# Trunk of a hybrid encoder: repeated key columns kept in scratch, load and copy order at the attention's start, norm statistics and input casts moved

## The chip, the cores and the metric

The kernel runs on one core of one Trainium2 chip. The metric is device time in microseconds (us) of one execution; the time before is the median of three runs. All times below are from the profile of one execution, from its trace, or from those runs.

## What is computed

One transformer layer runs on two sequences with shared weights: a prompt of 1024 tokens (s=0) and a sample of 512 tokens (s=1), each with 16 meta tokens ahead of it (n = 1040 and 528). The width is 1024, all in 32-bit floats.

```python
def mixer_sublayer(x, ...):
    n = rms_norm(x, g_mix)
    qa, ka, va, qb, kb, vb = jnp.split(n @ w_in, cuts, axis=-1)
    # group A: 8 query heads on 2 key heads of 64, RMS-normed q and k, axial rotary
    oa = softmax(rope(norm(qa)) @ rope(norm(ka)).T * scale) @ va
    # group B: 4 heads, difference of two softmax maps, linear rotary, v of 128
    p  = softmax(qb @ kb.T * scale)                  # two maps per head
    ob = rms_norm((p[0] - lam * p[1]) @ vb, g_subln) * (1 - lam_init)
    return x + concat(oa, ob) @ w_out
def conv_glu_sublayer(x, ...):
    n = rms_norm(x, g_ffn)
    gate = depthwise_conv3(n @ w_ff_gate) + conv_b
    return x + (gelu(gate) * (n @ w_ff_up)) @ w_ff_down
# a last RMSNorm, and the meta tokens are dropped
```

## The kernel before

Every dense product (`dense`, `mm3` at L132 to L134) is three matmuls of split operands: the rounded high part of the data by the high weights, the low part by the high weights, the high part by the low weights. `split` and `load_weight` (L126, L127) make the parts: a cast on ACT (or POOL, L153) gives `_hi`, a subtraction on DVE or POOL gives `_lo`. Weights stream in as `w_f` tiles of 128x1024 on ACT's DMA queue; all other loads and stores are issued by SP, in order.

The program is a set of Python generators that a scheduling function, `merge`, interleaves by weights: `projection(s)` (norm statistics, q, k and v with rotary, stores to scratch in HBM: `qk`, `ka`, `v`, `vt`), `attention(s)` (group A in blocks of 512 queries, then group B in blocks of about 342 or 306 and 208), `mixer_out(s)` (w_out, residual, sum of squares) and `conv_glu(s)`. The stages are: the sample's projection alone; the sample's attention beside the prompt's projection (`R1`, with a lead of `LEAD1` for the projection); the prompt's attention beside the sample's feed-forward (`f1`, `R2`); the prompt's `mixer_out` beside the rest of `f1` (`R3`); the prompt's `conv_glu` alone. Each engine then works through its own list in order: an instruction that waits holds up all that stands behind it on that engine.

Names and places in this text:

- `load_k` (L378, L394): loads 1040 key columns. A softmax reads `nch` equal chunks of an even width `kw`, 3x348 = 1044 columns for the prompt, so POOL copies the first four columns behind the last (L394). For the sample 2x264 = 528 needs no copy.
- `load_q` (L378), `load_v` (L399, and `v_tail`, L401): q, v and the last rows of v. In group A, POOL copies the first two columns of a head's first q block into `halo` (L512).
- `softmax`: scores `ps_s` (L413, L414 on PE), a scale with a running minimum into `p` (L417, DVE), exp (L420, ACT). In group B ACT scales both maps, with the factor `c` from POOL for the second (L545, then L546), and POOL adds them into `p` (L547). `pt_hi` and `pt_lo` are the transposed p (L434 on PE, L126 and L127), multiplied by v at L444 to L448 and L458.
- In `projection`: `x` loads (L193), `xhi` (L195, ACT), `xlo` (L196, DVE), squares (L199, ACT). The prompt's squares are summed into `acc` by POOL (L204), then L214 (PE) and `rsqrt_newton` (L113 to L119) give `rstd`. POOL multiplies the rotary tables by `rstd` (L347); `head_norm` adds `eps2` (L234, POOL) ahead of a matmul (L238).
- In `mixer_out`: `h<-oT` loads (L629), casts `xhi<-h` (L126; L636 on POOL for the sample), the residual add, a square (L589, ACT) and the running sum `acc` (L590, POOL); at the end the mean by a matmul with `ones_d` (L595, PE).

Of the kernel before, what the change touches and what calls it, by code (L numbers as in the profile page):

```python
# [51 lines left out]
def even_chunks(total, cap):  # L52
    cnt = -(-total // cap)
    w = -(-total // cnt)
    w += w % 2
    out, c = [], 0
    while c < total:
        out.append((c, min(w, total - c)))
        c += w
    return out  # L60

# [68 lines left out]
def mm3(g, ps, whi, wlo, xhi, xlo, start, stop):  # L130
    nc = g.nc
    nc.tensor.matmul(ps, lhsT=whi, rhs=xhi, start=start, stop=False)  # L132
    nc.tensor.matmul(ps, lhsT=whi, rhs=xlo, start=False, stop=False)  # L133
    nc.tensor.matmul(ps, lhsT=wlo, rhs=xhi, start=False, stop=stop)  # L134
# [25 lines left out]
def projection(ctx, g, s, side, tag, tag2):  # L160
# [23 lines left out]
    with tc.tile_pool(name=f"ps{s}", bufs=2, side=side, reuse_waits="tile") as sp:  # L184
        if s == 1:
            ms = [g.psum.tile(P, cw, tag2) for _, cw in chunks]
        else:
            acc = sp.tile([P, n], F32, name="acc", bufs=1)
        for k in range(KT):
            for c0, cw in even_chunks(n, 528):  # L190
                cc = slice(c0, c0 + cw)
                x = g.xin.tile([P, 528], F32, name="x", tag="x")[:, :cw]
                nc.sync.dma_start(out=x, in_=g.xT[s][k * P:(k + 1) * P, cc])  # L193
                gk = g.vec[:, V_GMIX + k:V_GMIX + k + 1]
                nc.scalar.activation(xhi[k][:, cc], x, AF.Copy, scale=gk)  # L195
                nc.vector.scalar_tensor_tensor(out=xlo[k][:, cc], in0=x, scalar=gk,  # L196
                                               in1=xhi[k][:, cc].bitcast(F32), op0=ALU.mult, op1=ALU.subtract)
                sq = acc[:, cc] if k == 0 and s == 0 else x
                nc.scalar.activation(sq, x, AF.Square)  # L199
                if s == 1:  # L200
                    for ps, (c1, w) in zip(ms, chunks):
                        nc.tensor.matmul(ps, lhsT=g.ones_d, rhs=x[:, c1:c1 + w], start=k == 0, stop=k == KT - 1)
                elif k:
                    nc.gpsimd.tensor_tensor(out=acc[:, cc], in0=acc[:, cc], in1=x, op=ALU.add)  # L204
        yield 0
        c0, cw = chunks[0]
        first_ps = g.psum.tile(P, cw, tag)
        dense(g, first_ps, first, xhi, xlo, c0, cw)
        for i, (c0, cw) in enumerate(chunks):
            if s == 1:  # L210
                ps = ms[i]
            else:
                ps = g.psum.tile(P, cw, tag2)
                nc.tensor.matmul(ps, lhsT=g.ones_d, rhs=acc[:, c0:c0 + cw], start=True, stop=True)  # L214
            nc.vector.tensor_scalar(out=eps2[:, c0:c0 + cw], in0=ps, scalar1=EPS, scalar2=2 * EPS,
                                    op0=ALU.add, op1=ALU.mult)
            rsqrt_newton(g, sp, rstd[:, c0:c0 + cw], ps, cw)
        nc.vector.tensor_scalar(out=rstd, in0=rstd, scalar1=-0.5, scalar2=None, op0=ALU.mult)
# [3 lines left out]
    tab = load_tables(0)  # L222
# [19 lines left out]
    def finish(y, hn, dst, twice, c0, cw):  # L242

        if hn is not None:
            nc.vector.tensor_tensor(out=y, in0=y, in1=hn[:, None, :].broadcast_to(list(y.shape)), op=ALU.mult)
        hi = tmp(bp, "hi", y.shape[1], cw, 2, F32R)
        lo = y.bitcast(F32R)
        split(g, hi, lo, y, nc.gpsimd)
        for i, part in enumerate((hi, lo, hi) if twice else (hi, lo)):
            to = dst[i, :, :, c0:c0 + cw]  # L250
            to = to.rearrange("x p n -> p x n") if y.shape[1] == 2 else to.rearrange("x p n -> (x p) n")[:, None]
            nc.sync.dma_start(out=to, in_=part.bitcast(F32))

    def pair(j, w=None):
# [4 lines left out]
        for c0, cw in chunks:  # L259
# [16 lines left out]
            finish(y, hn, g.qk[s][PAIRS.index(j)], QB <= j < KB, c0, cw)  # L276

    def keys_a():
        cos, sin = tab
        gk, ngk = scales[KA]  # L280
        for c0, cw in chunks:
            cc = slice(c0, c0 + cw)
            if c0 == 0:
# [14 lines left out]
            finish(y, head_norm(sq, g.ones_hd, c0, cw, HD), g.ka[s], True, c0, cw)  # L298
            yield 25 * cw

    def values(j):
        w = load_weight(g, g.w_in[j], lo_engine=nc.gpsimd)
        dst, tail = g.v[s][0 if j == VA else 1 + j - VB], g.vt[s][0 if j == VA else 1 + j - VB]
        for c0, cw in chunks:
# [11 lines left out]
            for i0, i1, kw in ((0, nf, P), (nf, nt, cw - nf * P)):  # L316
# [11 lines left out]
                if kw == P:  # L328
                    nc.sync.dma_start(out=dst[:, t0 + i0:t0 + i1, :], in_=v.bitcast(F32)[:, i0:i1, :])
# [27 lines left out]
def attention(ctx, g, s, side):  # L357
# [3 lines left out]

    nch = -(-n // 512)
    kw = -(-n // nch)
    kw += kw % 2
# [25 lines left out]
    def load_k(j, m, first=0):  # L390
        k = kp.tile([P, ne], F32R, name="k", tag="k")
        stacked(k[:, :n], j, m, first, 0, n)
        if ne > n:
            nc.gpsimd.tensor_copy(k[:, n:], k[:, :ne - n])  # L394
        return k

    def load_v(i, w, c0):
        v = vp.tile([P, nf, 2 * P], F32R, name="v", tag="v")[:, :, :w]
        nc.sync.dma_start(out=v.bitcast(F32), in_=g.v[s][i][:, :, c0:c0 + w])  # L399
# [181 lines left out]
def add_square(g, tp, acc, h, j, c0, cw, eng, bufs=2):  # L581
# [5 lines left out]
    else:  # L587
        sq = tp.tile([P, cw], F32, name="sq", tag="sq", bufs=bufs)
        nc.scalar.activation(sq, hs, AF.Square)  # L589
        eng.tensor_tensor(out=acc, in0=acc, in1=sq, op=ALU.add)  # L590


def mean_rsqrt(g, tp, out, acc, cw, tag="mm"):
    ps = g.psum.tile(P, cw, tag)
    g.nc.tensor.matmul(ps, lhsT=g.ones_d, rhs=acc, start=True, stop=True)  # L595
# [3 lines left out]
def mixer_out(g, s, st, side, whole, tag):  # L599
# [6 lines left out]
    with ExitStack() as es:  # L606
        mp = pool(es, g, f"fm{s}", 3, side)
        waiting = []

        def finish():  # L610
            while waiting:
                c0, cw, acc = waiting.pop(0)
                mean_rsqrt(g, mp, rstd[:, c0:c0 + cw], acc, cw, tag)

        for group in ([chunks] if whole else [[c] for c in chunks]):
            if whole:
                (xhi, xlo), base = [[x[:, k] for k in range(KT)] for x in st.x], 0
            else:
                xhi = [mp.tile([P, cm], F32R, name="xhi", tag=f"xhi{k}", bufs=2) for k in range(KT)]
                xlo = [mp.tile([P, cm], F32R, name="xlo", tag=f"xlo{k}", bufs=2) for k in range(KT)]  # L620
# [19 lines left out]
            for j in range(KT):  # L640
                w = load_weight(g, g.w_out[j])
                for c0, cw in group:
# [9 lines left out]
                    add_square(g, mp, acc[:, c0 - base:c0 - base + cw], h, j, c0, cw, nc.gpsimd, 1)  # L652
# [127 lines left out]
def merge(a, wa, b, wb, lead=0, tail=False):  # L780
# [4 lines left out]
    while True:  # L785
        i = 0 if b is None or done[0] / wa <= done[1] / wb else 1
        try:
            w = next((a, b)[i])
# [23 lines left out]
LEAD1, LATE = 2 * 24 * 384, 22  # L812
# [3 lines left out]
def trunk_kernel(ctx, tc, g):  # L816
# [5 lines left out]
    for s, N in enumerate(SEQS):  # L822
        n = N + NMETA
        g.qk.append([dram.tile([3, 2, P, n], F32, name=f"qk{s}_{i}") for i in range(len(PAIRS))])
        g.ka.append(dram.tile([3, 2, HD, n], F32, name=f"ka{s}"))
        g.v.append([dram.tile([P, n // P, 2 * P], F32, name=f"v{s}_{i}") for i in range(5)])
# [70 lines left out]
    with ExitStack() as es:  # L897
        g.xin = pool(es, g, "xin", 7, "right")
# [4 lines left out]
    with es0:  # L903
        with ExitStack() as es1:
            merge(attention(es1, g, 1, "right"), R1[0], p0, R1[1], LEAD1)
# [4 lines left out]
    with ExitStack() as es1:  # L910
# [6 lines left out]
        with ExitStack() as es0:  # L917
# [3 lines left out]
            merge(a0, R2[0], f1, R2[1], tail=True)  # L921
        g.psum.relay(s=6)
        st0 = state(ctx, 0, "left", False)
        merge(mixer_out(g, 0, st0, "left", False, "s"), R3[0], f1, R3[1])
# [5 lines left out]
    drain(conv_glu(ctx, g, 0, st0, "right", 2))  # L930
# [64 lines left out]
```

## Time and profile before

| what | value |
|---|---|
| median of 3 runs | 2268.64 us (2266.8 to 2272.45) |
| profiled execution | 2269.33 us, its span in the trace 2267.5 us |
| TensorE clock granted, mean | 0.97 |
| PE (matmul) busy | 2130.6 us, 94% |
| DVE, ACT, POOL busy | 56%, 46%, 29% |
| DMA | 215.62 MB, mean 95 GB/s |

A busy share is an average over all stages. The span's last third (the prompt's feed-forward, from about 1500 us on) shows PE busy almost without a break; the idle time of PE lies in the start, at the changes of stage, and in group B of the prompt's attention. For each idle stretch the trace names the engine and instruction that ended it, and the same question can then be put to that engine.

### The profile page before, as it was taken

The numbers are of one execution on the slowest core, as the hardware profiler recorded it, in microseconds if no ns is written. First come the engines' busy times: TensorE is split into PE (matmuls) and PEld (weight loads), VectorE is DVE, ScalarE is ACT, GpSimd is POOL, SyncE is SP. The second block draws the span as 40 slices with busy tenths as digits, with TensorE's granted clock in tenths as the row PEclk, the third lists the DMA queues.
The fourth block names the chain that finished last, engine by engine and source line by source line (L and its number), as shares of the span: only waits on it lengthen the run. The fifth ranks groups of instructions, "written<-read, shape, count | busy, mean of one in ns | idle before, by whom it ended". The sixth has DMA issues, their size and how long they took to land.

```text
span 2267.5 us, 32349 instructions
## 1 busy us (share of the span) xinstructions
PE 2130.6 (94%) x12442; PEld 1916.5 (85%) x12442; DVE 1264.2 (56%) x2201; ACT 1038.8 (46%) x1830; POOL 664.3 (29%) x575
## 2 busy tenths in 40 slices
PE   6978999995999999999989987989999999999997
PEld 5977999884988888888879986988888888888887
DVE  5636554453577667676757764774433444433445
ACT  5525555564565455466757775542122211122224
POOL 3763355440432112243333432531111001111004
PEclk8999999997999999999999998999999999999999
DMA  6563334444322222223323214631111111111112
GB/s 211 184 215 104 123 122 147 155 146 145 98 70 74 90 72 72 81 85 104 107 78 101 87 49 132 207 106 47 38 56 48 48 48 52 40 45 56 47 38 75
DMA packets 107178, 215.62 MB, mean 95 GB/s; under 512 B 10640, under 2 KB 62864, under 8 KB 106512
## 3 DMA queue, kind: packets, MB, share of 16 engines
q1 hardware_dynamic: 78224, 108.69, 15.1%
q10 hardware_dynamic: 28800, 104.87, 14.4%
q8 instruction: 98, 1.61, 0.3%
q14 instruction: 56, 0.46, 0.1%
HBM read 167.37 MB, written 46.15 MB: 94 GB/s over the span
## 4 chain that ended last, share of the span: by engine, by line
PE 82%; DMA 7%; DVE 4%; ACT 2%; issue 2%; POOL 1%; SPq 1%; DVEq 0%; POOLq 0%; ACTq 0%
PE ps_mm L132 19%; PE ps_mm L133 19%; PE ps_mm L134 19%; PE ps_t L434 5%; PE ps_s L413 4%; PE ps_s L414 3%; DMA k<-qk 2%; DMA q<-qk 2%; PE ps_o L449 2%; PE ps_o L448 2%; PE ps_p L132 1%; PE ps_p L134 1%; PE ps_p L133 1%; PE ps_o L444 1%; PE ps_o L446 1%
## 5 line engine op out<-in xcount | busy, mean ns | idle before, releaser
L132 PE MATMUL ps_mm<-xhi,w_hi 128*128 128x512 f32 (+6 forms) x1968 | 663.3, 337 | 8.7 <-POOL xhi L636 8.6
L133 PE MATMUL ps_mm<-xlo,w_hi 128*128 128x512 f32 (+6 forms) x1968 | 657.8, 334 | 1.4 <-POOL xlo L127 1.4
L134 PE MATMUL ps_mm<-xhi,w_lo 128*128 128x512 f32 (+6 forms) x1968 | 658.0, 334 | 0.0
L132 PEld LDWEIGHTS ps_mm<-xhi,w_hi 128*128 128x128 f32 x1968 | 373.6, 190 | 34.3 <-POOL xhi L636 8.9
L133 PEld LDWEIGHTS ps_mm<-xlo,w_hi 128*128 128x128 f32 x1968 | 372.8, 189 | 26.6 <-POOL xlo L127 2.0
L134 PEld LDWEIGHTS ps_mm<-xhi,w_lo 128*128 128x128 f32 x1968 | 372.4, 189 | 25.2 <-issue 0.2
L126 ACT CAST w_hi<-w_f 128x1024 fp32r<-128x1024 f32 x134 | 139.1, 1047 | 406.5 <-PE ps_mm L133 363.8
L417 DVE TENSOR_SCALAR_CACHE_REDUCE p<-ps_s 114x1044 f32<-114x1044 f32 (+5 forms) x212 | 223.3, 1054 | 139.8 <-PE ps_s L414 101.9
L127 POOL TENSOR_TENSOR a_lo<-gate,a_hi 128x512 fp32r<-128x512 f32 x66 | 97.1, 1472 | 652.8 <-ACT a_hi L126 648.8
L420 ACT ACTIVATE p<-p,nm 114x1040 f32<-114x1040 f32 (+5 forms) x212 | 215.2, 1015 | 115.9 <-DVE p L417 115.0
L126 ACT CAST pt_hi<-ps_t 128x512 fp32r<-128x512 f32 (+6 forms) x360 | 169.2, 483 | 206.0 <-PE ps_t L434 180.5
L726 DVE TENSOR_TENSOR h<-ps_mm,h 128x512 f32<-128x512 f32 (+1 forms) x288 | 182.3, 645 | 126.1 <-PE ps_mm L134 124.4
L127 DVE TENSOR_TENSOR pt_lo<-ps_t,pt_hi 128x512 fp32r<-128x512 f32 (+4 forms) x312 | 171.9, 563 | 124.5 <-ACT pt_hi L126 122.4
L413 PE MATMUL ps_s<-k,q 128*114 128x348 f32 (+4 forms) x552 | 183.7, 338 | 38.8 <-DVE p L417 30.0
L133 PE MATMUL ps_mm<-a_lo,w_hi 128*128 128x512 f32 (+1 forms) x576 | 216.7, 379 | 3.3 <-POOL a_lo L127 3.3
L134 PE MATMUL ps_mm<-a_hi,w_lo 128*128 128x512 f32 (+1 forms) x576 | 216.1, 378 | 0.0
L132 PE MATMUL ps_mm<-a_hi,w_hi 128*128 128x512 f32 (+1 forms) x576 | 215.8, 386 | 0.0
L434 PE MATMUL ps_t<-ident,p 128*128 128x128 f32 (+7 forms) x1188 | 185.2, 272 | 5.0 <-POOL p L547 3.7
L127 DVE TENSOR_TENSOR w_lo<-w_f,w_hi 128x1024 fp32r<-128x1024 f32 x106 | 136.1, 1292 | 87.1 <-ACT w_hi L126 86.9
L414 PE MATMUL ps_s<-k,q 128*114 128x348 f32 (+4 forms) x552 | 175.0, 323 | 3.5 <-DMA q<-qk 3.5
L434 PEld LDWEIGHTS ps_t<-ident,p 128*128 128x128 f32 (+7 forms) x1188 | 144.1, 138 | 33.1 <-issue 7.0
L714 DVE TENSOR_TENSOR gate<-ps_mm,gate 128x512 f32<-128x512 f32 x66 | 45.5, 690 | 189.4 <-PE ps_mm L134 186.6
(197 smaller groups left out, 3583.6 us busy)
## 6 DMA issues: line engine op xcount, KB each, us to landing
w_f<-w_gate ACTq DMA_DIRECT2D x44, 512.0 KB
w_f<-w_up ACTq DMA_DIRECT2D x44, 512.0 KB
w_f<-w_down ACTq DMA_DIRECT2D x44, 512.0 KB
w_f<-w_in ACTq DMA_DIRECT2D x36, 512.0 KB
w_f<-w_out ACTq DMA_DIRECT2D x32, 512.0 KB
q<-qk SPq DMA_DIRECT2D x48, 171.0 KB
qk<-hi SPq DMA_DIRECT2D x16, 384.0 KB
qk<-y SPq DMA_DIRECT2D x12, 384.0 KB
```

What stands on the lines that cost most here:

```text
L126: nc.scalar.copy(hi, src)
L127: (lo_engine or nc.vector).tensor_tensor(out=lo, in0=src, in1=hi.bitcast(F32), op=ALU.subtract)
L132: nc.tensor.matmul(ps, lhsT=whi, rhs=xhi, start=start, stop=False)
L133: nc.tensor.matmul(ps, lhsT=whi, rhs=xlo, start=False, stop=False)
L134: nc.tensor.matmul(ps, lhsT=wlo, rhs=xhi, start=False, stop=stop)
L413: nc.tensor.matmul(ps[:, i], lhsT=qk[0][0], rhs=qk[0][1][:, kc], start=True, stop=False)
L414: nc.tensor.matmul(ps[:, i], lhsT=qk[1][0], rhs=qk[1][1][:, kc], start=False, stop=True)
L417: nc.vector.tensor_scalar(out=p.rearrange("p (i w) -> p i w", i=nch), in0=ps, scalar1=-HD ** -0.5, scalar2=3.0e38, op0=ALU.mult, op1=ALU.m ...
L420: nc.scalar.activation(p, p, AF.Exp, bias=nm, scale=-1.0, accum_out=l)
L434: nc.tensor.transpose(tps[:, c:c + M], p[:, k0:k0 + kw], g.ident[:M, :M])
L714: nc.vector.tensor_tensor(out=a, in0=up, in1=a, op=ALU.mult)
L726: nc.vector.tensor_tensor(out=hs, in0=ps, in1=hs, op=ALU.add)
```

## The change

1. `qk` and `ka` in scratch are 1044 columns wide for the prompt. When the first chunk of a key pair is stored, `finish` stores its first four columns a second time behind the last (7 small stores of SP). `load_k` loads 1044 columns, and the 12 copies on POOL are gone.
2. In group A, the `halo` copy stands behind the four softmaxes of its block, not ahead of them, and the v load is issued behind the first q load.
3. A's v lies in scratch as two contiguous blocks, one for each key head; each store of it becomes two.
4. The prompt's projection: the input pool has 8 buffers, not 7; no `first_ps`; the statistics are computed ahead of the first `yield` and with high priority, so its x loads, casts, squares and POOL adds move from the 75 to 160 us of before into the sample's projection; its tables are loaded behind its last x. `LEAD1` is one chunk instead of two, and attention's first work is issued behind the last matmul of the lead. In PE's list the first scores stand behind one such chunk (24 matmuls of 384 columns) in both kernels; the six statistics matmuls (L214) that stood there are gone from that place.
5. `mean_rsqrt` can take a pair: the last square of `mixer_out` goes to PE as a second matmul, not to POOL.
6. `mixer_out(0)`: 12 shared buffers each for `xhi` and `xlo` instead of 2 for each of 8; it yields ahead of its last chunk, and the caller starts `conv_glu(0)` before it ends.
7. The build has a parameter `dynamic_dma_scratch_size=1024`.

```diff
@@ projection
-                nc.sync.dma_start(out=x, in_=g.xT[s][k * P:(k + 1) * P, cc])
+                load = nc.sync.dma_start(out=x, in_=g.xT[s][k * P:(k + 1) * P, cc]).ins
...
-        yield 0
         c0, cw = chunks[0]
-        first_ps = g.psum.tile(P, cw, tag)
-        dense(g, first_ps, first, xhi, xlo, c0, cw)
-        for i, (c0, cw) in enumerate(chunks):
+        if s == 1:
+            first_ps = g.psum.tile(P, cw, tag)
+            dense(g, first_ps, first, xhi, xlo, c0, cw)
+        with tc.high_priority() if s == 0 else nullcontext():
+            for i, (c0, cw) in enumerate(chunks):
...
+    with tc.issue_after(load) if s == 0 else nullcontext():
+        tab = load_tables(0)
+    yield 0
@@ finish (projection)
+            if keys and c0 == 0 and ne > n:
+                to = dst[i, :, :, n:]
...
+                nc.sync.dma_start(out=to, in_=part.bitcast(F32)[:, :, :ne - n])
@@ values
+                    if j == VA:
+                        for m in range(2):
+                            nc.sync.dma_start(out=dst[m, :, tt, :], in_=v.bitcast(F32)[:, i0:i1, m * P:(m + 1) * P])
@@ attention
-        stacked(k[:, :n], j, m, first, 0, n)
-        if ne > n:
-            nc.gpsimd.tensor_copy(k[:, n:], k[:, :ne - n])
+        stacked(k, j, m, first, 0, ne)
...
-        v = load_v(0, P, kv * P)
+        v = None
...
+                v = v or load_v(0, P, kv * P)
                 if kv + h + b == 0:
                     yield 0
-                if lead:
-                    nc.gpsimd.tensor_copy(halo[:, 2 * i:2 * i + 2], q[:, :2])
...
                     yield 2 * n
+                if lead:
+                    nc.gpsimd.tensor_copy(halo[:, 2 * i:2 * i + 2], q[:, :2])
@@ add_square, mean_rsqrt, mixer_out
+        if eng is None:
+            return sq
...
-    g.nc.tensor.matmul(ps, lhsT=g.ones_d, rhs=acc, start=True, stop=True)
+    parts = acc if isinstance(acc, tuple) else (acc,)
+    for i, part in enumerate(parts):
+        g.nc.tensor.matmul(ps, lhsT=g.ones_d, rhs=part, start=i == 0, stop=i == len(parts) - 1)
...
-                xhi = [mp.tile([P, cm], F32R, name="xhi", tag=f"xhi{k}", bufs=2) for k in range(KT)]
-                xlo = [mp.tile([P, cm], F32R, name="xlo", tag=f"xlo{k}", bufs=2) for k in range(KT)]
+                if group[0] == chunks[-1]:
+                    yield None
+                xhi = [mp.tile([P, cm], F32R, name="xhi", tag="xhi", bufs=12) for k in range(KT)]
+                xlo = [mp.tile([P, cm], F32R, name="xlo", tag="xlo", bufs=12) for k in range(KT)]
@@ merge, trunk_kernel
+            with g.tc.issue_after(g.mark) if lead and not i else nullcontext():
+                w = next((a, b)[i])
+            lead = lead if i else 0
...
-LEAD1, LATE = 2 * 24 * 384, 22
+LEAD1, LATE = 24 * 384, 22
...
-        g.xin = pool(es, g, "xin", 7, "right")
+        g.xin = pool(es, g, "xin", 8, "right")
...
+    f0 = conv_glu(ctx, g, 0, st0, "right", 2)
+    next(f0)
+    for _ in range(ML + 2):
+        next(m0)
+    next(f0)
+    drain(m0)
```

POOL in group B of the prompt's attention, around the first pair of key copies of one head (`a_lo` is the feed-forward's low part, `w_hi` a weight cast). Before:

```order
343 L153 CAST w_hi<-w_f 128x1024
344 L547 TENSOR_TENSOR p<-p 114x1040
345 L127 TENSOR_TENSOR a_lo<-gate,a_hi 128x512
346 L153 CAST w_hi<-w_f 128x1024
347 L545 TENSOR_TENSOR c<-r_b,neglam 114x1
348 L127 TENSOR_TENSOR a_lo<-gate,a_hi 128x512
349 L547 TENSOR_TENSOR p<-p 114x1040
350 L394 COPY k<-k 128x4
351 L545 TENSOR_TENSOR c<-r_b,neglam 114x1
352 L394 COPY k<-k 128x4
353 L547 TENSOR_TENSOR p<-p 114x1040
```

And in the changed kernel (its line numbers are its own: L565 is L545, L567 is L547, L134 is L127):

```order
331 L160 CAST w_hi<-w_f 128x1024
332 L567 TENSOR_TENSOR p<-p 114x1040
333 L134 TENSOR_TENSOR a_lo<-gate,a_hi 128x512
334 L160 CAST w_hi<-w_f 128x1024
335 L565 TENSOR_TENSOR c<-r_b,neglam 114x1
336 L134 TENSOR_TENSOR a_lo<-gate,a_hi 128x512
337 L567 TENSOR_TENSOR p<-p 114x1040
338 L565 TENSOR_TENSOR c<-r_b,neglam 114x1
339 L567 TENSOR_TENSOR p<-p 114x1040
```

Only the two copies are gone; the rest keeps its order.

ACT at the start of the prompt's `mixer_out`, behind the last block of attention (the casts `xhi<-h` of the first chunk are 128x344, of the second 128x342). Before:

```order
1243 L116 ACTIVATE o_rs<-rs_y 128x342
1244 L126 CAST xhi<-h 128x344 x3
1245 L126 CAST xhi<-h 128x342 x7
1246 L586 ACTIVATE acc<-h 128x256
1247 L589 ACTIVATE sq<-h 128x256 x2
1248 L126 CAST xhi<-h 128x342
1249 L589 ACTIVATE sq<-h 128x256
1250 L126 CAST w_hi<-w_f 128x1024
```

In the changed kernel:

```order
1275 L123 ACTIVATE o_rs<-rs_y 128x342
1276 L133 CAST xhi<-h 128x344 x3
1277 L133 CAST xhi<-h 128x342 x4
1278 L133 CAST w_hi<-w_f 128x1024
1279 L606 ACTIVATE acc<-h 128x344
1280 L156 DMA w_f<-w_out 128x1024
```

Four casts of the second chunk now stand ahead of the weight cast, not eight, and the squares of the sample's feed-forward (128x256) are no longer here.

POOL in the sample's projection. Before:

```order
9 L127 TENSOR_TENSOR w_lo<-w_f,w_hi 128x1024
10 L234 TENSOR_TENSOR sq<-sq,eps_179 64x256
11 L127 TENSOR_TENSOR w_lo<-w_f,w_hi 128x1024
12 L347 TENSOR_TENSOR rope<-rope,rstd 128x528 x2
13 L234 TENSOR_TENSOR sq<-sq,eps_179 64x272
```

In the changed kernel:

```order
9 L134 TENSOR_TENSOR w_lo<-w_f,w_hi 128x1024
10 L245 TENSOR_TENSOR sq<-sq,eps_179 64x256
11 L211 TENSOR_TENSOR acc<-acc,x 128x520 x2
12 L134 TENSOR_TENSOR w_lo<-w_f,w_hi 128x1024
13 L211 TENSOR_TENSOR acc<-acc,x 128x520 x6
14 L371 TENSOR_TENSOR rope<-rope,rstd 128x528 x2
15 L211 TENSOR_TENSOR acc<-acc,x 128x520 x2
16 L245 TENSOR_TENSOR sq<-sq,eps_179 64x272
```

Eight of the prompt's adds now stand ahead of the tables' multiplication by `rstd`. On SP all 16 x loads of the prompt go out ahead of the sample's first `ka` store; before, seven did.

More of the change, by code (lines that the diff above doesn't have):

```diff
@@ L1 @@
-from contextlib import ExitStack
+from contextlib import ExitStack, nullcontext
 import numpy as np
@@ L133, in mm3 @@
     nc.tensor.matmul(ps, lhsT=whi, rhs=xlo, start=False, stop=False)
-    nc.tensor.matmul(ps, lhsT=wlo, rhs=xhi, start=False, stop=stop)
+    g.mark = nc.tensor.matmul(ps, lhsT=wlo, rhs=xhi, start=False, stop=stop).ins
 def dense(g, ps, w, xhi, xlo, c0, cw, order=range(KT)):
@@ L240, in head_norm, with finish @@
         return ps
-    def finish(y, hn, dst, twice, c0, cw):
+    nch, kw_ = key_chunks(n)
+    ne = nch * kw_
+    def finish(y, hn, dst, keys, twice, c0, cw):
         if hn is not None:
@@ L282, in keys_a @@
             cc = slice(c0, c0 + cw)
[L283 removed]
+            if c0 == 0 and s == 1:
                 ps = first_ps
@@ L651, in mixer_out @@
                     nc.vector.tensor_tensor(out=h[:, j, c0:c0 + cw], in0=ps, in1=res, op=ALU.add)
-                    add_square(g, mp, acc[:, c0 - base:c0 - base + cw], h, j, c0, cw, nc.gpsimd, 1)
+                    last = j == KT - 1 and c0 + cw == C
+                    sq = add_square(g, mp, acc[:, c0 - base:c0 - base + cw], h, j, c0, cw, None if last else nc.gpsimd, 1)
                     yield 24 * cw
```

63 lines of the change are left out of this document (35 added, 28 removed).

## The prediction

> **What bounds the kernel now.** I read the page's busy shares and its chain first: PE does the work, and the chain that ended last runs on PE for 82% of the span.
>
> ```profile
> PE 2130.6 (94%) x12442; PEld 1916.5 (85%) x12442; DVE 1264.2 (56%) x2201; ACT 1038.8 (46%) x1830; POOL 664.3 (29%) x575
> PE 82%; DMA 7%; DVE 4%; ACT 2%; issue 2%; POOL 1%; SPq 1%; DVEq 0%; POOLq 0%; ACTq 0%
> ```
>
> The change removes hardly any PE work, so it can only win PE's idle time, at most 6% of the span. The view of waits says for whom PE waited (total us, times, longest):
>
> ```profile
> PE ps_s L413 <- DVE p L417: 30.0, 24, 5.4
> PE ps_s L132 <- ACT w_hi L126: 8.9, 3, 8.2
> PE ps_s L413 <- DMA q<-qk: 8.9, 3, 6.6
> PE ps_mm L132 <- POOL xhi L636: 8.6, 1, 8.6
> PE ps_p L132 <- DVE z L295: 7.7, 1, 7.7
> PE ps_o L444 <- ACT pt_hi L126: 7.6, 2, 6.3
> PE ps_s L595 <- POOL acc L590: 6.1, 1, 6.1
> PE ps_t L434 <- POOL p L547: 3.7, 1, 3.7
> PE ps_mm L133 <- POOL a_lo L127: 3.3, 2, 2.5
> PE ps_mm L238 <- POOL sq L234: 3.1, 1, 3.1
> ```
>
> Few long waits, each at a place of its own. For each I asked what its releaser had waited for. In group B and at the start of the prompt's attention the answer on POOL's timeline is the key copy, which waits for its DMA with the real work queued behind it:
>
> ```profile
> 515.97 0.19 POOL L394 CAST k<-k 128x4 fp32r<-128x4 f32 x1 [7.20 <-DMA k<-ka]
> ...
> 521.65 0.19 POOL L394 CAST k<-k 128x4 fp32r<-128x4 f32 x1 [5.34 <-DMA k<-ka]
> 521.80 1.29 POOL L547 TENSOR_TENSOR p<-p 102x528 f32<-102x528 f32 x1
> ...
> 960.07 0.19 POOL L394 CAST k<-k 128x4 fp32r<-128x4 f32 x1 [5.08 <-DMA k<-qk]
> ...
> 1169.87 0.19 POOL L394 CAST k<-k 128x4 fp32r<-128x4 f32 x1 [8.40 <-DMA k<-qk]
> 1170.01 2.37 POOL L547 TENSOR_TENSOR p<-p 114x1040 f32<-114x1040 f32 x1
> ```
>
> PE stands behind them, in its own timeline:
>
> ```profile
> 517.35 0.54 PE L444 MATMUL ps_o<-pt_hi,v 128*128 128x208 f32 x1 [6.25 <-ACT pt_hi L126]
> ...
> 523.15 0.43 PE L434 MATMUL ps_t<-ident,p 102*128 102x102 f32 x1 [3.67 <-POOL p L547]
> ...
> 528.52 0.66 PE L413 MATMUL ps_s<-k,q 128*128 128x348 f32 x1 [0.34 <-DMA q<-qk]
> ...
> 962.51 0.80 PE L133 MATMUL ps_mm<-a_lo,w_hi 128*128 128x512 f32 x1 [2.51 <-POOL a_lo L127]
> ...
> 963.53 0.63 PE L133 MATMUL ps_mm<-a_lo,w_hi 128*128 128x512 f32 x1
> 963.96 0.63 PE L134 MATMUL ps_mm<-a_hi,w_lo 128*128 128x512 f32 x1
> ...
> 1075.49 0.64 PE L413 MATMUL ps_s<-k,q 128*114 128x348 f32 x1 [3.19 <-DVE p L417]
> ...
> 1167.74 0.40 PE L133 MATMUL ps_mm<-a_lo,w_hi 128*128 128x512 f32 x1
> 1167.97 0.39 PE L134 MATMUL ps_mm<-a_hi,w_lo 128*128 128x512 f32 x1
> 1173.73 0.64 PE L413 MATMUL ps_s<-k,q 128*114 128x348 f32 x1 [5.36 <-DVE p L417]
> ```
>
> A second thing is seen here. In undisturbed work 512-column matmuls start 0.23 us apart (1167.74, 1167.97); behind the 2.51 us wait they start 0.43 apart (963.53, 963.96). Such slow stretches last about 3 us in the timeline, so a wait of over 2 us costs about 1.5 us more (an estimate).
>
> **The terms.** The sum is made against the profiled execution's 2269.3 us; the median of the runs is 0.7 us lower.
>
> *Key copies in group B (940 to 1180 us): -12.* The loads for one head are issued a head ahead, so nothing but the copy needs them when they land. Named waits: a_lo 3.3 (two), pt_hi 7.6 less 6.3 = 1.3, and 3.19 and 5.36 for p, each behind a copy on POOL: 13.2. Of the two p waits the usual one stays (30.0 over 24 waits, 1.25 each): 10.7. Three of them are over 2 us, 1.5 each: 15.2. I keep 12, as some work then meets the next late engine (ACT and DVE share the softmax chain). Ends: 8 (half the waits reappear) and 16. The 7 small stores are SP issues off PE's path: 0.
>
> *Start of the prompt's attention (500 to 560 us): -4.* The copies go, so the sample's last block ends about 10 us earlier (6.25 and 3.67). But the first scores of the prompt need both k, landed at 521.65, and q. On SP:
>
> ```profile
> 504.90 12.86 SPq L401 DMA_DIRECT2D v_tail<-vt  x1
> ...
> 521.55 8.95 SPq L378 DMA_DIRECT2D q<-qk  x6
> ```
>
> q was issued at 521.55, behind a `v_tail` issue that took 12.86 us, and scores began at 528.52. In the changed kernel q takes v's slot, ahead of `v_tail`, and queues behind the k loads. It can be there between 521.65 and 528.5; I take 524.5, so 4 us of some 10 are kept. The wait of 8.6 us for `xhi` (the sample's `mixer_out`, behind its `h<-oT` loads) follows the same SP queue with the same bytes; I leave it. Ends: 0, if the queue drains no sooner, and 16: 521.65 for q (7) and the 8.6 wait as well.
>
> *Start of the sample's attention (157 to 180 us): -5.* Again two rows:
>
> ```profile
> 158.10 0.55 SPq L378 DMA_DIRECT2D q<-qk  x1
> ...
> 166.28 0.56 PE L413 MATMUL ps_s<-k,q 128*128 128x264 f32 x1 [6.62 <-DMA q<-qk]
> ```
>
> q took 8.2 us to be usable, behind v in the queue. It moves one and a half issues forward and v behind it: a gain between 1.3 (the same 8.2) and 6.6 (the whole wait). I take 3. The halo copies no longer hold `sq` (3.1 us, L238); the usual chain keeps one of these: 2. Ends 0 and 9. The statistics matmuls leave this place but are done at another: 0.
>
> *Casts at the prompt's `mixer_out`: -8.* ACT's timeline:
>
> ```profile
> 1397.48 0.48 ACT L126 CAST xhi<-h 128x342 fp32r<-128x342 f32 x1 [2.65 <-DMA h<-oT]
> ...
> 1398.18 1.03 ACT L126 CAST w_hi<-w_f 128x1024 fp32r<-128x1024 f32 x1
> ```
>
> The weight cast that PE waited 8.2 us for stood behind a cast of the second chunk, which waited for attention's last store to come back. With 12 buffers only four such casts stand ahead, and the sample's squares are gone from there; those squares now sit in attention's last blocks. About 1.5 us of the wait stays, and a slow stretch goes. Ends 4 and 10. What comes in its place: with 12 buffers the next chunk's last four casts wait for the current chunk's last reads: +1, ends 0 and 4.
>
> *Last square by PE: -3.5.* POOL's two last adds:
>
> ```profile
> 1500.15 1.17 POOL L590 TENSOR_TENSOR acc<-acc,sq 128x340 f32<-128x340 f32 x1
> 1501.92 1.24 POOL L590 TENSOR_TENSOR acc<-acc,sq 128x340 f32<-128x340 f32 x1 [0.60 <-ACT sq L589]
> ```
>
> The wait was 6.1 us; the last add (1.24) and its hand-over go, one matmul comes (about 0.7 us cold), and the ACT square with its residual add remains ahead. Without the POOL adds behind one another (1500.15, 1501.92) PE starts some 2.5 us sooner, and 1 of the slow stretch goes. Ends 2 and 4.5.
>
> *The first 60 us: +2.* Rows of ACT and POOL, and the group of the adds (min/median/max in ns, then first and last start):
>
> ```profile
> 21.39 0.74 ACT L195 ACTIVATE xhi<-x,vec 128x528 fp32r<-128x528 f32 x1 [0.90 <-DMA x<-xT]
> ```
> ```profile
> 40.09 2.57 POOL L347 TENSOR_TENSOR rope<-rope,rstd 128x528 f32<-128x528 f32 x2 [4.29 <-DVE rstd L218]
> ```
> ```profile
> L204 POOL TENSOR_TENSOR acc<-acc,x x14: 1292/1317/2292, 87.2 to 130.8; 128x520 f32<-128x520 f32 x14
> ```
>
> The sample's last x came at 21.39, behind four table loads in the SP queue; ahead of them it comes some 3 us sooner. Against that, `z` (L295, PE waits 7.7 for it) needs the tables times `rstd`, and eight adds of 1.317 us, 10.5 us, now stand ahead of that on POOL, and several casts and squares of the prompt on ACT ahead of the `rstd` chain. POOL has the 4.29 free just there and more before, so most of it fits if the x loads arrive. Ends -6 and +12. The leaving of these adds from 87 to 131 us wins nothing: PE did not wait for them.
>
> *A's contiguous v, the second store of each, the pool parameter: 0.* The stores are off the path, and the v load still writes the same rows of SBUF.
>
> Sum: -12 - 4 - 5 - 8 + 1 - 3.5 + 2 = -29.5, so 2239.8 in the profile and 2239 for the median.
>
> **A page against the row.** The Trainium skill ("TensorE: Matmul & The Clock Gate", section "Why this matters for your kernels") says that PE drops to its lower clock only after idle gaps of more than about 3 us. By that only the longest of the three group B waits would bring a slow stretch, and 3 us fewer would be won there: an estimate of 2242. The rows differ: the matmuls behind 2.51 us ran at half pace, so I keep 1.5 for each.
>
> **Rivals.** *DMA sets both starts of attention.* k and q land no sooner, so those two terms are zero: 2269.3 - 20.5 = 2249. For it: 12.86 us in one issue, a full queue. Against: q passes v in both places.
>
> *More of it pays.* q comes at the best end in both places and the `xhi` wait goes too, since the sample's last `oT` store now goes out ahead of `v_tail`: 16 and 9 in place of 4 and 5, so 2224. Against: the second pair of k and v loads still stands ahead of `h<-oT`.
>
> *The start is crowded.* POOL's 10.5 us and ACT's added work fall on the `z` chain, with 3 us gained on the last x and some overlap lost: +14, not +2, so 2252.
>
> *Slower.* One mechanism decides: 16 x loads ahead of the first `ka` store, with 8 buffers, each freed only after ACT's square and POOL's add. If the 14 adds go at the pace of before (130.8 - 87.2 = 43.6 us for them) and what PE needs stands behind all of them, the start costs 43.6 and the rest wins 31.5: 2281. It decides from 38 us of loss on. Against: at the pace of before POOL had other work between the adds.
>
> *The copies weren't the cause.* If k were needed as it lands, group B would keep its waits (12 lost: 2252); but the first use of those keys is the next head.
>
> **How the numbers follow.** Forecast as summed, 0.42; DMA sets both starts 0.24; more pays 0.18; crowded start 0.09; copies not the cause 0.03; slower 0.04. The range of 8 in 10 leaves out the slow case and the worst of the middle ones above, and the best of the good case below: 2218 to 2258. The forecast's own range is 2230 to 2246. A change under 0.3% (7 us) can't be told from none: faster, below 2262, has 0.89 (all but the slow case and part of the crowded and DMA ones, where both come together); within, 0.06; slower, 0.05.
>
> **What would show it.** On POOL no key copy, and no a_lo or p wait over 2 us on PE between 940 and 1180. The first scores of the prompt some 4 us sooner behind the k issue than before. At the prompt's `mixer_out` a wait for `w_hi` under 3 us; at the end of it a wait of about 3 us for an ACT square. Wrong would be: the wait for `z` in the first 60 us grown past 12 us, scores that wait for k where POOL waited before, or new breaks between the chunks of `mixer_out`.

## The result

The changed kernel takes 2237.4 us (median of 4 runs, 2231.6 to 2239.7) against 2268.1 before: the ratio is 0.9858, 95% interval 0.9835 to 0.988. The forecast was 2239. The sum came out nearly right, but not by its terms: group B won almost twice what was forecast, and neither start of attention left a gain in the end. Of the kernel with part 4 undone, shown below, one run of four took 4864 us; its ratio leaves that run out, and its median of 2238.9 us is 2238.4 without it.

The first lines of the changed kernel's page, and its view of PE's waits (in its own line numbers: L432 and L433 are the scores, L139 to L141 the dense products, L314 is `z`, L663 the sample's `xhi`, L619 the mean):

```profile
span 2235.6 us, 32340 instructions
PE 2118.3 (95%) x12446; PEld 1909.4 (85%) x12446; DVE 1259.3 (56%) x2201; ACT 1035.4 (46%) x1830; POOL 658.8 (29%) x561
```

```profile
PE ps_s L432 <- DVE p L436: 20.8, 21, 2.4
PE ps_p L139 <- DVE z L314: 16.7, 1, 16.7
PE ps_s L432 <- DMA q<-qk: 14.0, 2, 12.3
...
PE ps_mm L139 <- POOL xhi L663: 11.3, 1, 11.3
...
PE ps_s L432 <- DMA qk<-hi: 3.7, 1, 3.7
...
PE ps_s L619 <- POOL acc L612: 2.1, 1, 2.1
PE ps_mm L249 <- POOL sq L245: 2.0, 1, 2.0
```

Gone are the waits for `w_hi`, `a_lo` and POOL's `p`, and the long waits for DVE's `p`. Three have grown: `z` from 7.7 to 16.7, the prompt's first q from 0.3 to 12.3, `xhi` from 8.6 to 11.3.

Where the time went is read from the start of the same matmul in both traces (us from the span's start):

| matmul | before | after | gain so far |
|---|---|---|---|
| first one behind the wait for `z` | 41.5 | 49.2 | -7.8 |
| sample's first score | 166.3 | 166.2 | 0.1 |
| prompt's first score | 528.5 | 524.8 | 3.7 |
| sample's `mixer_out`, first | 566.2 | 566.9 | -0.6 |
| one score before group B's waits | 909.4 | 910.2 | -0.8 |
| one score behind them | 1252.4 | 1231.9 | 20.5 |
| prompt's `mixer_out`, last | 1496.8 | 1470.8 | 26.1 |
| prompt's `conv_glu`, first | 1504.0 | 1474.2 | 29.8 |
| last of all | 2257.8 | 2226.1 | 31.7 |

The gains are taken before rounding.

### The profile page after: what moved, and what is told of

It is laid out like the page before. It is cut to its first block, busy times and chain, and to the rows that moved or that the text cites. A ratio compares the mean times of both kernels' runs of the same rounds, so it can differ in the third digit from the quotient of the medians.

```text
span 2235.6 us, 32340 instructions
## 1 busy us (share of the span) xinstructions
PE 2118.3 (95%) x12446; PEld 1909.4 (85%) x12446; DVE 1259.3 (56%) x2201; ACT 1035.4 (46%) x1830; POOL 658.8 (29%) x561
## 4 chain that ended last, share of the span: by engine, by line
PE 86%; DVE 4%; DMA 4%; ACT 2%; issue 1%; POOL 1%; SPq 0%; DVEq 0%; ACTq 0%; POOLq 0%
PE ps_mm L139 20%; PE ps_mm L140 20%; PE ps_mm L141 20%; PE ps_t L453 5%; PE ps_s L432 4%; PE ps_s L433 4%; DMA q<-qk 2%; PE ps_o L468 2%; PE ps_o L467 2%; PE ps_p L139 1%; PE ps_p L140 1%; PE ps_p L141 1%; PE ps_o L463 1%; PE ps_o L464 1%; PE ps_o L465 1%
## 5 line engine op out<-in xcount | busy, mean ns | idle before, releaser
L139 PE MATMUL ps_mm<-xhi,w_hi 128*128 128x512 f32 (+6 forms) x1968 | 663.2, 337 | 11.3 <-POOL xhi L663 11.3
L141 PE MATMUL ps_mm<-xhi,w_lo 128*128 128x512 f32 (+6 forms) x1968 | 656.9, 334 | 0.0
L139 PEld LDWEIGHTS ps_mm<-xhi,w_hi 128*128 128x128 f32 x1968 | 372.9, 190 | 36.7 <-POOL xhi L663 11.6
L141 PEld LDWEIGHTS ps_mm<-xhi,w_lo 128*128 128x128 f32 x1968 | 371.9, 189 | 24.8
L134 POOL TENSOR_TENSOR a_lo<-gate,a_hi 128x512 fp32r<-128x512 f32 x66 | 97.7, 1481 | 654.0 <-ACT a_hi L133 650.0
L134 DVE TENSOR_TENSOR pt_lo<-ps_t,pt_hi 128x512 fp32r<-128x512 f32 (+4 forms) x312 | 172.0, 564 | 110.6 <-ACT pt_hi L133 107.2
L432 PE MATMUL ps_s<-k,q 128*114 128x348 f32 (+4 forms) x552 | 181.5, 335 | 38.5 <-DVE p L436 20.8
L139 PE MATMUL ps_mm<-a_hi,w_hi 128*128 128x512 f32 (+1 forms) x576 | 216.2, 387 | 0.0
L141 PE MATMUL ps_mm<-a_hi,w_lo 128*128 128x512 f32 (+1 forms) x576 | 215.7, 377 | 0.0
L134 DVE TENSOR_TENSOR w_lo<-w_f,w_hi 128x1024 fp32r<-128x1024 f32 x106 | 133.7, 1269 | 85.5 <-ACT w_hi L133 85.3
L433 PE MATMUL ps_s<-k,q 128*114 128x348 f32 (+4 forms) x552 | 173.4, 320 | 3.1 <-DMA q<-qk 3.1
```

Of the source, the lines that this page charges most:

```text
L134: (lo_engine or nc.vector).tensor_tensor(out=lo, in0=src, in1=hi.bitcast(F32), op=ALU.subtract)
L141: g.mark = nc.tensor.matmul(ps, lhsT=wlo, rhs=xhi, start=False, stop=stop).ins
L432: nc.tensor.matmul(ps[:, i], lhsT=qk[0][0], rhs=qk[0][1][:, kc], start=True, stop=False)
L433: nc.tensor.matmul(ps[:, i], lhsT=qk[1][0], rhs=qk[1][1][:, kc], start=False, stop=True)
```

## The experiments

Each ratio is to the kernel before, measured beside it; the changed kernel's 0.9858 is to be compared with them. The median of the kernel before was 2265.2, 2265.5 or 2268.4 us beside these runs and 2268.1 beside the changed kernel, so a few us between times of different sets mean nothing.

### Part 1 alone

```diff
 (the kernel before)
-        stacked(k[:, :n], j, m, first, 0, n)
-        if ne > n:
-            nc.gpsimd.tensor_copy(k[:, n:], k[:, :ne - n])
+        stacked(k, j, m, first, 0, ne)
 (and the wider scratch, with the second store of four columns)
```

> The kernel before with part 1 of the change alone: the repeated key columns are stored in scratch, the 12 POOL copies are gone. Theory (the copies held POOL, and through it ACT and PE): the stretch from the prompt's score group at 910 us to the one at 1250 us gets 20 us shorter, as in the changed kernel (21.3 there), and the whole time is about 2247; the waits for w_hi (8.2) and for POOL's last add (6.1) stay. Rival (the copies were worth only the 12 us that the prediction priced, and the rest of the 21 came from another part of the change): about 2256.

2249.3 us, ratio 0.9918 (0.9903 to 0.9933): 19 of the changed kernel's 31 us, and all of it in group B. Between the two scores of the table the kernel before needs 343.0 us, this one 323.3, the changed one 321.7. The view by windows shows that stretch, before, with this edit, and in the changed kernel (span of the window, busy PE, PEld, DVE, ACT, POOL, then PE's clock):

```profile
909.37:1252.40 343.03, 325.87 (x1968) 292.58 (x1967) 234.81 (x396) 218.43 (x355) 118.79 (x103) 0.97 0.30 93
```
```profile
909.64:1232.89 323.25, 318.82 (x1968) 287.71 (x1967) 233.86 (x396) 217.64 (x355) 118.88 (x97) 0.99 0.32 99
```
```profile
910.22:1231.90 321.68, 317.26 (x1969) 286.33 (x1967) 233.64 (x396) 217.70 (x355) 118.83 (x97) 1.00 0.33 100
```

PE's idle time falls from 17.2 (343.03 - 325.87) to 4.4, that is 12.7; and the same matmuls take 7.1 to 8.6 us less PE time, as the granted clock goes from 0.97 to 0.99 and 1.00. At the start of the prompt's attention nothing is won: the sample's last block ends sooner, and PE waits for q instead.

```profile
528.46 0.63 PE L423 MATMUL ps_s<-k,q 128*128 128x348 f32 x1 [12.63 <-DMA q<-qk]
```

In the kernel before, that score started at 528.52.

### The wait for z

DVE's timeline in the changed kernel (L203 is the prompt's `xlo`, L124 and L126 the `rstd` chain, L314 `z`), and POOL's beside it:

```profile
29.76 2.26 DVE L203 SCALAR_TENSOR_TENSOR xlo<-x,vec,xhi 128x520 fp32r<-128x520 f32 x3
...
38.24 6.87 DVE L203 SCALAR_TENSOR_TENSOR xlo<-x,vec,xhi 128x520 fp32r<-128x520 f32 x4
45.03 0.50 DVE L124 SCALAR_TENSOR_TENSOR ps_t<-ps_t,eps,rstd 128x272 f32<-128x272 f32 x1
...
48.20 0.49 DVE L314 SCALAR_TENSOR_TENSOR z<-ps_p,negain,rope 64x256 f32<-64x256 f32 x1
```
```profile
37.20 10.30 POOL L211 TENSOR_TENSOR acc<-acc,x 128x520 f32<-128x520 f32 x6
47.87 2.57 POOL L371 TENSOR_TENSOR rope<-rope,rstd 128x528 f32<-128x528 f32 x2 [0.37 <-DVE rstd L227]
```

Four `xlo` of the prompt stand directly ahead of the last part of the `rstd` chain and of `z` on DVE, and took 1.7 us each while POOL's adds ran; three others had taken 0.75 each. Three kernels moved this work:

```diff
 (a: the changed kernel, xlo behind the z of the sample's last key chunk)
+                with tc.issue_after(g.zmark) if s == 0 else nullcontext():
                     nc.vector.scalar_tensor_tensor(out=xlo[k][:, cc], ...)
 (b: only POOL's adds, behind the multiplication of the sample's tables)
+                    with tc.issue_after(g.tabmark):
                         nc.gpsimd.tensor_tensor(out=acc[:, cc], ...)
 (c: as a, but behind the sample's first query pair)
```

(a) 

> The changed kernel, with the prompt's xlo subtractions on DVE issued behind the sample's z of its last key chunk (and with them the squares and POOL adds of the prompt). Theory (the wait for z grew from 7.7 to 16.7 because the prompt's xlo stand ahead of the rstd chain and of z in DVE's list): the wait is 8 or less again, and the time falls by 8 to 10 us against the changed kernel, to about 2228. Rival (ACT's added casts and squares delay the rstd chain): the wait stays over 12 and the time within 4 us of 2237.

(b) 

> The changed kernel, with only the prompt's POOL adds issued behind the multiplication of the sample's tables; eight xlo subtractions stay ahead of the rstd chain on DVE. Theory (DVE's subtractions run at 1.7 us instead of 0.76 while POOL's adds run beside them): the xlo at 32 to 46 us take about 0.8 us each, the wait for z is 10 to 13 us, the time about 2232. Rival 1 (POOL's adds themselves stand in the chain): the wait is back at 8 and the time is that of the kernel with xlo behind z. Rival 2 (the order on DVE alone, contention nothing): xlo stay at 1.7 us, the wait at 15 to 17, the time at 2237.

(c) 

> The changed kernel, with the prompt's xlo on DVE (and with them its squares and adds) issued behind the sample's first query pair, some 35 us later than in the kernel with xlo behind z. Theory (this work costs PE time only where it meets the sample's short softening chains of the first 70 us; from 70 to 140 us DVE, ACT and POOL have room, as PE lost under 0.4 us per 20 us there): PE's loss up to 160 us falls from 33.5 to about 24, the last projection matmul ends near 149 instead of 157.7, the first score comes 8 us sooner, 2229. Rival 1 (the work costs the same wherever it stands, as with xlo behind z, which also lost 33.5): 2235 to 2240. Rival 2 (the first score hangs on q's store and load, not on PE): the projection ends sooner, the wait for q grows by the same, 2237.

(a) 2237.0 us, 0.9868 (0.9854 to 0.9883): no gain. The wait for `z` is gone, but PE loses the time at other places of the same chain:

```profile
37.81 1.27 PE L250 MATMUL ps_t<-sq,ones_hd 128*128 128x272 f32 x2 [5.03 <-POOL sq L246]
...
53.49 0.69 PE L334 MATMUL ps_t<-ident,t 128*128 128x128 f32 x2 [4.38 <-DVE y L261]
69.60 0.60 PE L139 MATMUL ps_p<-xhi,w_hi 128*128 128x272 f32 x1 [2.54 <-DVE t L328]
```

The last product of the sample's projection starts at 157.6 us; in the changed kernel it started at 157.9.

(b) 2243.2 us, 0.989 (0.9875 to 0.9905): its time was forecast wrong, and of its durations only those of `xlo` were right. With the adds moved behind, two `xlo` took 1.42 us together and `z` came at 40.9 instead of 48.2; PE no longer waits for it, but 9.2 us at `sq` (POOL, behind ACT) and later 3.2 and 5.3. An `xlo` at 33.64 still took 1.79 us, beside a `w_lo` subtraction of POOL.

```profile
37.04 1.42 DVE L203 SCALAR_TENSOR_TENSOR xlo<-x,vec,xhi 128x520 fp32r<-128x520 f32 x2
...
40.88 0.49 DVE L315 SCALAR_TENSOR_TENSOR z<-ps_p,negain,rope 64x256 f32<-64x256 f32 x1
...
48.40 8.54 DVE L203 SCALAR_TENSOR_TENSOR xlo<-x,vec,xhi 128x520 fp32r<-128x520 f32 x1 [0.35 <-ACT xhi L202]
```

(c) 2245.1 us, 0.9911 (0.9892 to 0.9929): slower than the changed kernel, against the theory. Its PE waits 5.06 us at 32 for `sq`, as in (a), then 5.06 us at 67 and 7.92 at 117, both for DVE:

```profile
125.09 0.59 PE L139 MATMUL ps_p<-xhi,w_hi 128*128 128x272 f32 x1 [7.92 <-DVE z L291]
```
```profile
124.28 0.42 DVE L289 SCALAR_TENSOR_TENSOR y<-ps_p,rope 128x256 f32<-128x256 f32 x1 [13.04 <-DMA qk<-y]
```

At 67 DVE was busy with eight `xlo` of the prompt (10.95 us together). At 117 it had nothing to do: it stood idle for 13.04 us until a store of `y` had landed. That store is issued by SP, which from 105.35 us on had issued the sample's four k loads; the section "Together" returns to this.

So the place of this work sets where PE waits, and its price did not fall in any of the three. The idle room on DVE and POOL between 70 and 140 us was no sign that it would be free there; in (c) the larger wait is not one for work on DVE, but for a store.

### Parts 2 and 4 undone

```diff
 (the changed kernel, part 2 undone)
-        v = None
+        v = load_v(0, P, kv * P)
 (and the halo copy ahead of the softmaxes)
```

> The changed kernel with part 2 undone: v loaded ahead of the first q again, and the halo copies ahead of the softmaxes. Theory (with k's four engines as the limit, q's place in the queue brings the prompt's first score sooner but the wait for xhi returns it; at the sample's start it is worth the 3 to 5 us by which the wait for q fell): 2240 to 2243, the prompt's first score 3 to 5 us later, the wait for xhi 3 to 5 us shorter. Rival (part 2 is worth nothing anywhere): 2235 to 2239. Second rival (worth what the prediction gave, 9): 2246.

2242.9 us, 0.9901 (0.9886 to 0.9916): the time of the first theory, though the prompt's score moved more and the wait for `xhi` less than it said. The sample's first score is 1.6 us later, the prompt's 6.7 us; the wait for `xhi` shrinks from 11.3 to 8.7 and takes part of that back, and 3.2 us are lost in group B. Part 2 is worth about 5 us by the times, and 10 by the ratios.

```diff
 (the changed kernel, part 4 undone)
-        with tc.high_priority() if s == 0 else nullcontext():
...
-        g.xin = pool(es, g, "xin", 8, "right")
+        g.xin = pool(es, g, "xin", 7, "right")
...
-LEAD1, LATE = 24 * 384, 22
+LEAD1, LATE = 2 * 24 * 384, 22
```

> The changed kernel with part 4 undone: the prompt's x work back in its old place in the code, seven input buffers, the old lead. Theory (part 4 lost 7.8 us at the wait for z and won about as much between there and the sample's first score): the wait for z back at 8, the first score at 165 to 167, the whole time 2235 to 2239. Rival 1 (part 4 costs its 8 us in full): 2229. Rival 2 (it wins on balance, by the statistics that no longer stand at the sample's first scores): 2243 or more.

2238.9 us, 0.988 (0.9863 to 0.9896): part 4 can't be told from nothing. But the wait for `z` did not go back to 8; it was 13.1, with 5.5 for `rstd` ahead of it, and the sample's first score came 2.8 us later than in the changed kernel. So this kernel does not restore the start of before, and the two halves of part 4 (a loss at `z`, a gain by the first score) are not separated.

### Buffers of mixer_out

```diff
 (the changed kernel)
-                xhi = [mp.tile([P, cm], F32R, name="xhi", tag="xhi", bufs=12) for k in range(KT)]
+                xhi = [mp.tile([P, cm], F32R, name="xhi", tag=f"xhi{k}", bufs=2) for k in range(KT)]
 (and xlo likewise)
```

> The changed kernel, with xhi and xlo of the prompt's mixer_out back in two buffers for each of eight k. ACT's list then has eight casts of the second chunk ahead of the first weight cast again, as before the change; the sample's squares stay where the change put them. Theory (those casts, behind the last store of attention, held w_hi): the wait for w_hi at the start of mixer_out is 5 to 8 us and the time about 2243. Rival (the squares and the rest of the sample's feed-forward, now in attention's last blocks, were the cause): the wait stays under 2 and the time at 2237.

2236.2 us, 0.987 (0.9853 to 0.9887): the rival. ACT's cast does wait for attention's last store, even longer than before, and the weight cast stands behind it, yet PE waits 0.95 us for it:

```profile
1383.48 0.48 ACT L133 CAST xhi<-h 128x342 fp32r<-128x342 f32 x1 [6.86 <-DMA h<-oT]
1383.87 1.04 ACT L133 CAST w_hi<-w_f 128x1024 fp32r<-128x1024 f32 x1
```
```profile
1384.96 0.43 PE L139 MATMUL ps_s<-xhi,w_hi 128*128 128x344 f32 x1 [0.95 <-ACT w_hi L133]
```

So the 12 buffers are not what took the 8.2 us away. What the traces show in their place is how much work PE had in hand: in the kernel before it ran 24 matmuls of `mixer_out`, those of one weight tile, and then stood at the blocked `w_hi`; here it runs 72, those of three, and is busy until 1384.0. That more weight tiles were ready because the sample's feed-forward had left this place is likely, but was not tried alone and stays open.

### How k and q are loaded

A k load moves 128 rows of 4176 bytes, its source laid out as 4 blocks of 32 rows. In the trace's packet records the 256 packets of the prompt's first two k loads take from 503.7 to 521.5 us, with 4 or fewer in flight (begun and not yet ended) for 17.1 of these 17.8 us and 3.2 on average. The Trainium skill ("DMA: Bandwidth & Descriptors", section "Why a DMA increments its semaphore by 16 and not by 1") says that the number of engines of a load is the largest number up to 16 that divides the slowest dimension of its source and that of its destination. By it these loads, with 4 and 128, run on 4 engines; the packets in flight agree, though that there were just 4 is inferred from them. The cut makes the two dimensions 32 and 32:

```diff
 (k alone, or k and q)
-        nc.sync.dma_start(out=tl.bitcast(F32), in_=parts[:, m, :, c0:c0 + cw])
+        for i in range(4):
+            nc.sync.dma_start(out=tl[i * 32:(i + 1) * 32].bitcast(F32), in_=parts[i, m, :, c0:c0 + cw])
```

Only k, in the changed kernel:

> The changed kernel, with every k load cut into four loads of 32 partitions. Theory (the first prompt scores wait 12.3 us because a k load keeps to four of the 16 DMA engines: 256 packets of 4176 bytes in about 17 us): the packets spread over 16 engines, both k and q are there within 8 us of the issue, the wait for q falls below 4 us, and the first prompt score comes 8 to 12 us sooner; if the wait of 11.3 for xhi shrinks as well (its loads stand behind the same queue), the time is 2217 to 2225. Rival (the shared queue of all stores and v is full, not the four engines): the first score moves less than 3 us. Second rival: the score comes sooner but the wait for xhi takes it back, 2235 to 2238.

k and q, in the changed kernel:

> The changed kernel, with every k load and every q load cut into four loads of 32 partitions. Theory (q keeps to four DMA engines as well): the waits for q of 3.7 (sample), 2.4 (at 400 us) and 5.4 (prompt) that were left with only k cut shrink to 1 to 2, and the time falls to about 2219, 7 under the kernel with only k cut. Rival (SP issues three more instructions of 0.5 us for each q, 312 in all, and stores behind them come late): the time is that of the kernel with only k cut, 2227, or more.

k and q, in the kernel before, its copies kept:

> The kernel before with nothing changed but k and q loads cut into four pieces; POOL's key copies stay. Theory (the copies cost what they do because k lands late, 8 to 20 us after its issue; with k on 16 engines POOL waits 2 to 4 us in each): most of group B's 21 us comes back without part 1, and with the faster q and k at the starts of attention the time is about 2225. Rival (copies hold POOL because they stand ahead of the next work whatever the load takes): group B keeps its waits, 2240.

Only k: 2227.0 us, 0.9815 (0.9799 to 0.9832). The wait for q falls from 12.3 to 5.4, that for `xhi` from 11.3 to 5.8.

k and q: 2204.0 us, 0.9727 (0.971 to 0.9745), 33 us under the changed kernel by the times and 30 by the ratios. Up to 17 packets of k are in flight, and the two loads take 9.2 us instead of 17.8. The prompt's first score starts at 501.9, and the wait for `xhi` is no longer in the list; a wait of 9.2 us for `o_b`, behind 1300 us, is new, and its cause stays open:

```profile
PE ps_p L139 <- DVE z L314: 16.7, 1, 16.7
PE ps_o L464 <- DVE o_b L580: 14.8, 2, 9.2
PE ps_s L433 <- DVE p L437: 12.1, 17, 1.8
...
PE ps_s L433 <- DMA q<-qk: 4.0, 1, 4.0
```

The cut also changes the number of loads, and no run tried that alone. The trace of the changed kernel speaks for the shape: one single load of v at 267.5 us, on the same queue, with 128 rows of 4096 bytes from a source of 128 rows, took 2.8 us with up to 19 packets in flight, where single k loads (128 rows of 4176 bytes) took 8.3 us at 1140.5 and 6.3 us at 1151.3 with at most 6. What else was under way then differs.

In the kernel before: 2217.9 us, 0.9791 (0.9774 to 0.9807). This one edit is worth more than the whole change. All 12 copies are still there, but POOL now waits 27.1 us for their loads where it waited 84.9 us, and the waits in group B go. The copies before, then with this edit, and the stretch of group B:

```profile
L394 POOL CAST k<-k x12: 186/186/187, 516.0 to 1169.9; 128x4 fp32r<-128x4 f32 x12
its engine sat idle before it (us, times) until:
  DMA k<-qk: 58.6, 7
  DMA k<-ka: 26.3, 4
```
```profile
L395 POOL CAST k<-k x12: 182/186/1108, 502.2 to 1116.1; 128x4 fp32r<-128x4 f32 x12
its engine sat idle before it (us, times) until:
  DMA k<-qk: 16.8, 6
  DMA k<-ka: 10.3, 4
```
```profile
879.94:1196.78 316.84, 314.98 (x1945) 283.46 (x1944) 227.69 (x394) 219.61 (x355) 122.42 (x103) 1.00 0.32 100
```

The stretch of 343.0 us takes 316.8, and PE is idle in it for 1.9 us (17.2 before, 4.4 in the changed kernel); as it holds 23 matmuls fewer, the idle time is the better comparison. The copy was the place of the wait; its length was that of the load.

### Together

> The changed kernel with both: k loads in four pieces, and the prompt's xlo behind the sample's first query pair. Theory (independent causes): both gains add, 2227 less the 8 of the xlo alone, about 2219. Rival (the k loads win only because the sample's attention starts late): no more than 2227.

2221.3 us, 0.9803 (0.9783 to 0.9823), against 0.9815 with k alone: the intervals overlap, the gain is unclear. The wait of 7.92 at 117 us does not appear in this one: DVE's wait for the store of `y` there is 0.74 us instead of 13.04. The two kernels differ in the k loads alone, so it was the uncut k loads that held this store, and with it DVE and PE.

> The changed kernel with k and q loads in four pieces each and the prompt's xlo behind the sample's first query pair. Theory (the two causes add, as they did with only k cut: 2227 to 2221): 6 us under the 2204 of the kernel with both loads cut, about 2198. Rival (the gain of the later xlo came from the k loads' place in that order, as the xlo change alone was 8 us slower than the changed kernel): 2204 to 2212.

2201.8 us, 0.9719 (0.9705 to 0.9734), against 0.9727: no difference was shown. What beats both kernels is the cut of k and q, by 1.3% against the changed kernel (0.9727 to 0.9858, each to its own runs of the kernel before).

## Why the prediction was right, and where its steps were not

- *Key copies in group B*, -12: measured -21.3 (343.0 to 321.7), -20 with part 1 alone. The mechanism was right, the size was not. The waits that went, 12.7, fit the 10.7 of the sum. The slow stretches behind them were priced at 4.5 and were worth 7 to 9, by PE's busy time at the same matmuls. The choice to keep 12 of the worked-out 15.2, for work that meets the next late engine, was wrong as well: nothing of that kind showed. The Trainium skill ("TensorE: Matmul & The Clock Gate", section "Why this matters for your kernels") names PE-idle gaps of more than about 3 us as what brings the lower clock. The prediction's estimate by it, 3 us less, would have been further off; it also counted one such gap among the three where the 3.19 us wait makes a second. The trace does not agree with that limit: behind 2.51 us of idle time the matmuls already ran at half pace (0.43 us apart instead of 0.23).
- *Start of the prompt's attention*, -4: the first score did come 3.7 sooner, and the wait for `xhi`, left alone in the sum, grew from 8.6 to 11.3. From the sample's first score to its first `mixer_out` matmul 0.8 us were lost. The step that failed is "I leave it": the loads behind this wait did not come sooner with PE (`h<-oT` is issued at 560.1 us, 559.6 before, and the first `xhi` starts at 566.4, 565.8 before), so the wait takes the gain. The queue is seen on SP, where the store issues now stall:

```profile
501.68 1.24 SPq L399 DMA_DIRECT2D k<-ka  x2
503.01 0.55 SPq L399 DMA_DIRECT2D q<-qk  x1
503.65 0.56 SPq L418 DMA_DIRECT2D v<-v  x1
506.59 15.33 SPq L267 DMA_DIRECT2D qk<-hi  x2
```

- *Start*, +2, and *start of the sample's attention*, -5: 7.8 lost up to the wait for `z`, and 7.9 won from there to the first score: 0 together, where -3 was forecast. Three steps were wrong. `z` does not need the tables times `rstd` (those are of the second rotary, used later); it stands behind the `rstd` chain in DVE's list. POOL's idle time was counted as free, while its adds slowed DVE. And the leaving of the adds from 87 to 131 us was given nothing, as PE did not wait for them; but PE's waits for DVE between `z` and the first score fell from 4.0 to 0.7 us, more than its wait just ahead of that score did (6.6 to 3.7). Whether the adds or other work of the prompt that left did this, no run shows.
- *Casts at the prompt's `mixer_out`*, -8 and +1: from one score behind group B's waits to the last product of `mixer_out` 5.6 us were won. PE's idle time at `mixer_out` fell by 9.0 us (10.8 to 1.8), but in attention's tail, where the squares and other work of the sample's feed-forward went, it grew by 4.8 (12.8 to 17.6). The size was about right; the reason given (12 buffers) fell, and the squares' new place had been given no price.
- *Last square by PE*, -3.5, with 1 of it for the slow stretch: measured -3.8 up to the first product of `conv_glu`, and 1.9 more within the 15 matmuls behind it, where the slow stretch went. PE's wait went from 6.05 to 2.10, and the extra matmul took 0.3 of PE:

```profile
1473.19 0.84 PE L619 MATMUL ps_s<-acc,ones_d 128*128 128x340 f32 x2 [2.10 <-POOL acc L612]
1473.87 0.74 PE L619 MATMUL ps_s<-sq,ones_d 128*128 128x340 f32 x2
```

What the sum lost at the starts (3 and 5 us) and at the casts (1.4) group B paid back (9), with 2 from the last square. That the total came within 2 us of the forecast is luck: errors of 11 us on one side and 9 on the other cancelled.

## What to carry to other kernels

Where an engine waits for a transfer, ask first why the transfer takes so long: count its packets in flight, for a load that keeps to a few of the engines costs every waiter, and cutting it was worth more than taking single waiters away. A wait removed ahead of a transfer that keeps its own time only moves the wait; follow the queue to the next consumer before booking the gain. Idle time of DVE and POOL is not one store of free time: their work beside each other can take longer, the short chains of a start pay for it, and a store held up on SP's queue can leave them idle.

## What the runs showed of the hardware

- One subtraction of 128x520 on DVE took 0.71 to 0.76 us alone, 1.7 beside POOL's adds, and once 8.54 us (the row at 48.40 above) while POOL worked almost without a break. The Trainium skill ("GPSIMD Engine Reference", section "1. Specifications") names an SBUF interface that POOL shares with DVE, with contention for DVE instructions with two SBUF inputs; the traces agree, and the times above are the price here.
- Loads of the same bytes differed by a factor of two in time with the shape of their source and the number of loads: 17.8 us for two k loads of 4 blocks, 9.2 for the same in eight pieces of 32 rows, for some 0.5 us of SP's time per added instruction.
